# A hybrid decoder trunk on one core: the gate's product stays in PSUM, the output bias is added during the mixer, and the mixer's end is put in another order

## The chip, the core and the metric

The program runs on 1 core of one Trainium2 chip. The metric is device microseconds from the first to the last instruction and what lies around them, as the runs report it. The kernel before took 2048.25 us (median of 3 runs, 2047.78 to 2049.02).

The engines are named as the profile names them: PE is TensorE (matmuls; PEld its weight loads), DVE is VectorE, ACT is ScalarE, POOL is GpSimd, SP is SyncE. Each takes its instructions in order. DMAs are issued from SP, ACT and POOL.

## What is computed

A sequence of 256 tokens with 2048 channels, float32, goes through two layers and a final norm. The change touches only the token mixer of the first layer:

```python
def conv_module(h, w_in, b_in, dw, dw_b, ln_g, ln_b, w_out, b_out):
    u = h @ w_in + b_in
    a, gate = jnp.split(u, 2, axis=-1)
    v = a * jax.nn.sigmoid(gate)
    v = lax.conv_general_dilated(v, dw[:, None, :], ..., feature_group_count=D_MODEL) + dw_b
    v = layer_norm(v, ln_g, ln_b)
    v = jax.nn.silu(v)
    return v @ w_out + b_out
...
        if i % N_MIXERS == 0:
            x = x + conv_module(rms_norm(x, mix_norm[i]), ...)
        ...
        x = x + mlp(rms_norm(x, mlp_norm[i]), ...)
```

`w_in` is 2048 x 4096, `w_out` 2048 x 2048, and the depthwise convolution has 31 causal taps per channel. After the mixer come a dense MLP, a state-space layer with a gated output, and a second MLP.

## The kernel before

Weights are read from HBM in *steps* of 1 MB, three buffers deep (SP issues the DMAs, line 91), and a step is used in two *halves*. Each half is split into two float32r parts, `hi` on ScalarE (line 117) and `lo = raw - hi` on GpSimd or VectorE (line 119), with four buffers of each; `run_steps` writes the split of half h + 4 ahead of the products of half h. `after(n, fn)` puts work n halves later; `tick` counts.

**Input projection and gate.** `conv_in` makes 16 channel blocks c of 128 channels, four halves each. TensorE accumulates values and gate of a block, feature-major, in a PSUM tile `acc` (two of them), 24 products of 256 columns a half (`mm_g`, lines 204 to 206). From block 2 on the `lo` parts are GpSimd's. When a block is complete, `gate` (lines 419 to 431) multiplies by the token scale into an SBUF tile `ga` (VectorE, 424), takes the sigmoid in place (ScalarE, 425), and multiplies into the tile `vT` (VectorE, 426):

```python
nc.vector.tensor_tensor(out=t, in0=A, in1=self.rstdB.broadcast_to([P, 2, T]), op=ALU.mult)
nc.scalar.activation(t[:, 1, :], t[:, 1, :], AF.Sigmoid, bias=b_in[:, KB + c:KB + c + 1])
nc.vector.scalar_tensor_tensor(out=self.cblk(c), in0=t[:, 0, :], scalar=b_in[:, c:c + 1], in1=t[:, 1, :], ...)
```

**Depthwise taps.** Blocks 0 to 11 are convolved on VectorE, 30 instructions of 256 columns each (line 792 through `depthwise`, accumulator `cv` in PSUM), the first tap on ScalarE (498). Blocks 12 to 15 are *packed*: four shifted copies of the block (tile `R`, by DMA through HBM for 12 to 14, by 16 on-chip copies on lines 445 and 447 for 15) against tap matrices `wpk`, 32 small products a block on TensorE (463), result `pk`. `packed_taps` makes the tap matrices: 16 small copies into `dp` on VectorE (369), then one GpSimd product a block (376).

**Norm.** With a shift taken from blocks 0 to 3, the blocks are centred in groups of four (VectorE, 543), squared (ScalarE, 545), and summed over channels by small products into `stat` (TensorE, 510). `ln_totals` and `ln_finish` make mean and scale, hold TensorE with dummy products (`keep_warm`, line 184), and write the normalised blocks `z` and, through SiLU, the split pair `sT` (lines 604 to 610, `lo` on line 231) for the output projection.

**Output projection.** `conv_out` streams `w_out` (`mm_t`, lines 215 to 217). Ahead of its first half stands `pre`: `ln_finish`, then the bias `b_out` is loaded by one POOL DMA (624) and added to the residual x by four GpSimd instructions (627), and background work for the state-space layer is queued.

**What sets the order.** The instructions of each engine are put in order when the program is built, by a scheduler that goes by priority and its own estimates; `high_priority(URGENT)` puts one ahead, `behind(ins)` keeps one after another. On the chip every engine works that order off and waits at its head. The tags `t2` (three buffers), `ga`, `acc` and the 2 KB banks `ms` are shared by what carries them.

## Time and profile before

| | us |
|---|---|
| median of 3 runs | 2048.25 (2047.78 to 2049.02) |
| the profiled execution, its own time | 2047.59 |
| its span, first to last instruction | 2045.3 |
| TensorE busy in the span | 1991.8 (97%) |
| VectorE busy | 1426.7 (70%) |
| ScalarE busy | 943.5 (46%) |
| GpSimd busy | 325.9 (16%) |
| mean granted TensorE clock | 0.989 |

Matmuls are pipelined and their ends are modelled, so TensorE's busy share runs high: what is to be read is where it is idle, and what ended the idle time. [...] In lists of instructions the idle time of the engine just ahead of one stands in brackets, with the instruction that released it.

### The profile page before, as it was taken

To read this page: it belongs to the slowest core of one execution; us is meant where nothing else is said; L and a number is where in the kernel's file an instruction comes from. 1 tells how busy PE (TensorE), PEld (TensorE's weight loads), DVE (VectorE), ACT (ScalarE), POOL (GpSimd) and SP (SyncE) were. 2 spreads that over 40 slices of the span, in tenths; PEclk is the share of its full clock that TensorE was granted. 3 is DMA by queue.
4 is the path that set the end of the run, shared out by engine and by line. 5 is a ranking of instruction groups with operands and counts; after the bars stand their busy time and mean duration, and the time that the engine had idled before them with its cause. 6 is when DMAs were issued, how large, how long until landed. Compare 5 with 4: busy or idle time off the path is not lost.

```text
span 2045.3 us, 28886 instructions
## 1 busy us (share of the span) xinstructions
PE 1991.8 (97%) x11612; PEld 1695.5 (83%) x11612; DVE 1426.7 (70%) x1897; ACT 943.5 (46%) x1155; POOL 325.9 (16%) x266
## 2 busy tenths in 40 slices
PE   8999899999999999999998899999999999999998
PEld 8999687888888888888886688888888888888887
DVE  7999899976867777776558645566555555655555
ACT  4444455454444545454443354455444444544444
POOL 2988401100000212321013500000000000000000
PEclk9999999999999999999998899999999999999999
DMA  8667357766765778777898756665656566565653
GB/s 233 166 166 212 122 184 239 240 220 191 250 204 188 198 222 266 255 249 217 315 322 278 273 184 186 187 184 186 192 191 193 185 186 195 191 210 186 188 196 130
DMA packets 317301, 428.48 MB, mean 209 GB/s; under 512 B 10209, under 2 KB 211985, under 8 KB 313681
## 3 DMA queue, kind: packets, MB, share of 16 engines
q1 hardware_dynamic: 301120, 384.85, 60.0%
q0 software_dynamic: 12048, 37.41, 6.0%
q10 hardware_dynamic: 4000, 4.38, 0.7%
q8 instruction: 91, 1.49, 0.3%
q14 instruction: 42, 0.34, 0.0%
HBM read 400.08 MB, written 34.91 MB: 213 GB/s over the span
## 4 chain that ended last, share of the span: by engine, by line
PE 84%; DVE 12%; issue 2%; POOL 1%; DMA 1%; ACT 0%; SPq 0%; ACTq 0%; POOLq 0%; DVEq 0%
PE acc L194 23%; PE acc L215 15%; PE acc L217 14%; PE acc L216 14%; PE acc L195 11%; DVE cv L792 4%; PE acc L205 1%; PE acc L206 1%; PE acc L204 1%; DVE lo L119 1%; DVE S L783 1%; DVE vT L426 1%; DVE ws L783 1%; DMA raw<-in_conv_w_in_dram 0%; DVE wt L783 0%
## 5 line engine op out<-in xcount | busy, mean ns | idle before, releaser
L117 ACT ACTIVATE hi<-raw 128x1024 fp32r<-128x1024 f32 x672 | 711.5, 1060 | 960.0 <-PE acc L217 501.6
L119 DVE TENSOR_TENSOR lo<-raw,hi 128x1024 fp32r<-128x1024 f32 x596 | 729.1, 1224 | 520.1 <-ACT hi L117 519.3
L194 PE MATMUL acc<-hT,hi 128*128 128x512 f32 x2048 | 725.9, 399 | 3.8 <-DVE t L771 3.8
L195 PE MATMUL acc<-hT,lo 128*128 128x256 f32 x2048 | 575.5, 281 | 1.7 <-DVE lo L119 1.7
L194 PEld LDWEIGHTS acc<-hT,hi 128*128 128x128 f32 x2048 | 385.1, 188 | 99.4 <-issue 3.5
L195 PEld LDWEIGHTS acc<-hT,lo 128*128 128x128 f32 x2048 | 387.7, 189 | 3.2 <-DVE lo L119 2.3
L215 PE MATMUL acc<-hi,rT 128*128 128x512 f32 x992 | 387.5, 391 | 0.0
L216 PE MATMUL acc<-lo,rT 128*128 128x512 f32 x992 | 386.3, 389 | 0.0
L217 PE MATMUL acc<-hi,rT 128*128 128x512 f32 x992 | 386.2, 389 | 0.0
L215 PEld LDWEIGHTS acc<-hi,rT 128*128 128x128 f32 x992 | 186.2, 188 | 40.4 <-issue 1.8
L217 PEld LDWEIGHTS acc<-hi,rT 128*128 128x128 f32 x992 | 186.2, 188 | 39.1
L216 PEld LDWEIGHTS acc<-lo,rT 128*128 128x128 f32 x992 | 186.2, 188 | 38.1
L119 POOL TENSOR_TENSOR lo<-raw,hi 128x1024 fp32r<-128x1024 f32 x76 | 188.3, 2492 | 99.4 <-ACT hi L117 99.3
L204 PE MATMUL acc<-hT,hi 128*128 128x256 f32 x512 | 146.6, 287 | 1.4 <-ACT hi L117 1.4
L206 PE MATMUL acc<-hT,lo 128*128 128x256 f32 x512 | 146.0, 285 | 1.9 <-POOL lo L119 1.9
L205 PE MATMUL acc<-hT,hi 128*128 128x256 f32 x512 | 146.7, 287 | 0.0
L792 DVE SCALAR_TENSOR_TENSOR cv<-vT,dw,cv 128x256 f32<-128x256 f32 x348 | 142.1, 478 | 0.8
L783 DVE TENSOR_TENSOR x<-x,acc 128x1024 f32<-128x1024 f32 (+1 forms) x72 | 83.5, 1160 | 33.4 <-PE acc L217 23.0
L204 PEld LDWEIGHTS acc<-hT,hi 128*128 128x128 f32 x512 | 99.1, 194 | 4.2 <-issue 2.1
L206 PEld LDWEIGHTS acc<-hT,lo 128*128 128x128 f32 x512 | 99.2, 194 | 3.0 <-POOL lo L119 2.1
L215 PE MATMUL acc<-hi,yT 128*128 128x512 f32 x256 | 100.9, 394 | 0.0
L217 PE MATMUL acc<-hi,yT 128*128 128x512 f32 x256 | 100.4, 392 | 0.0
(265 smaller groups left out, 1778.2 us busy)
## 6 DMA issues: line engine op xcount, KB each, us to landing
raw<-in_mlp_w_up_dram SPq DMA_DIRECT2D x128, 1024.0 KB, 5.8
raw<-in_mlp_w_down_dram SPq DMA_DIRECT2D x128, 1024.0 KB, 5.2
raw<-in_ssm_w_glu_dram SPq DMA_DIRECT2D x32, 1024.0 KB, 5.5
raw<-in_conv_w_in_dram SPq DMA_DIRECT2D x60, 512.0 KB, 5.5
raw<-in_conv_w_out_dram SPq DMA_DIRECT2D x16, 1024.0 KB, 5.3
Vd<-bv POOLq DMA_DIRECT2D x16, 512.0 KB, 5.6
Md<-Kd POOLq DMA_DIRECT2D x32, 256.0 KB, 8.0
Wt<-Wd SPq DMA_DIRECT2D x8, 1024.0 KB, 7.8
```

What stands on the lines that cost most here:

```text
L117: self.nc.scalar.activation(hi, sl, AF.Copy)
L119: ins = eng.tensor_tensor(out=lo, in0=sl, in1=hi.bitcast(F32), op=ALU.subtract)
L194: mm(accs[m], lhsT=hi[:, kk, c], rhs=x, start=first and kk == 0, stop=False)
L195: mm(accs[m][:, 0:T], lhsT=lo[:, kk, c], rhs=x[:, 0, :], start=False, stop=last and kk == 3)
L204: mm(accs[m], lhsT=hi[:, kk, c], rhs=x[:, 0, :], start=first and kk == 0, stop=False)
L205: mm(accs[m], lhsT=hi[:, kk, c], rhs=x[:, 1, :], start=False, stop=False)
L206: mm(accs[m], lhsT=lo[:, kk, c], rhs=x[:, 0, :], start=False, stop=last and kk == 3)
L215: mm(acc[:, b, :], lhsT=ak[:, 0, t], rhs=hi[:, kk, :], start=first and kk == 0, stop=False)
L216: mm(acc[:, b, :], lhsT=ak[:, 0, t], rhs=lo[:, kk, :], start=False, stop=False)
L217: self.mm_last = mm(acc[:, b, :], lhsT=ak[:, 1, t], rhs=hi[:, kk, :], start=False, stop=last and kk == 1)
L783: self.nc.vector.tensor_tensor(out=out, in0=a, in1=b, op=op)
L792: return self.nc.vector.scalar_tensor_tensor(out=out, in0=a, scalar=s, in1=b, op0=op0, op1=op1)
```

## The change

- `gate` writes the scaled product back to its PSUM tile `acc`; the sigmoid goes from there to a tile `ga` of one block in SBUF, and the last instruction reads one operand from PSUM and one from SBUF.
- The 16 copies into `dp` go to ScalarE.
- The output bias is loaded in four pieces of 512 columns (tag `t2`) and added by GpSimd during the input projection, written at halves 20, 28, 36 and 44 (`add_b_out`), instead of ahead of the output projection.
- The 16 copies of block 15 are put in another order, six on ScalarE and ten on VectorE (before: ten and six), and go ahead of other work.
- Packed block 13 is written 8 halves after its gate, as block 12 is, instead of at the end. Block 14 and 15 stay at the end.
- Each packed block is evacuated and centred in one VectorE instruction; its square goes to ScalarE, and its two statistics products stand between the first 20 and the last 12 products of the next packed block. The centring of blocks 12 to 14 as a group goes. `ln_totals` stands within block 15's products.
- Dummy products: 3 and 9 instead of 5 and 11.

```diff
@@ packed_taps
+        self.sqs = {}
                 for g in range(4):
-                    nc.vector.tensor_copy(out=dp[32 * r:32 * r + 32, :, g, :],
-                                          in_=self.dw[32 * g:32 * g + 32, PACKED[0]:, r::4])
+                    nc.scalar.activation(dp[32 * r:32 * r + 32, :, g, :],
+                                         self.dw[32 * g:32 * g + 32, PACKED[0]:, r::4], AF.Copy)
...
+        for i in range(NS):
+            self.after(20 + 8 * i, lambda i=i: self.add_b_out(i))
+
+    def add_b_out(self, n):
+        nc = self.nc
+        s = slice(n * 512, (n + 1) * 512)
+        bo = self.t2([P, 512], name="bo")
+        nc.gpsimd.dma_start(out=bo, in_=self.a["conv_b_out"][:, s].broadcast_to([P, 512]))
+        with self.behind(self.pool_ins):
+            nc.gpsimd.tensor_tensor(out=self.x[:, :, s], in0=self.x[:, :, s],
+                                    in1=bo.unsqueeze(1).broadcast_to([P, NB, 512]), op=ALU.add)
@@ gate
-        t = self.tmp.tile([P, 2, T], F32, tag="ga", name="ga", bufs=2)
+        t = self.tmp.tile([P, T], F32, tag="ga", name="ga", bufs=2)
         with self.tc.high_priority(offset=URGENT):
-            nc.vector.tensor_tensor(out=t, in0=A, in1=self.rstdB.broadcast_to([P, 2, T]), op=ALU.mult)
-            nc.scalar.activation(t[:, 1, :], t[:, 1, :], AF.Sigmoid, bias=b_in[:, KB + c:KB + c + 1])
-            nc.vector.scalar_tensor_tensor(out=self.cblk(c), in0=t[:, 0, :], scalar=b_in[:, c:c + 1], in1=t[:, 1, :],
+            nc.vector.tensor_tensor(out=A, in0=A, in1=self.rstdB.broadcast_to([P, 2, T]), op=ALU.mult)
+            nc.scalar.activation(t, A[:, 1, :], AF.Sigmoid, bias=b_in[:, KB + c:KB + c + 1])
+            nc.vector.scalar_tensor_tensor(out=self.cblk(c), in0=A[:, 0, :], scalar=b_in[:, c:c + 1], in1=t,
                                            op0=ALU.add, op1=ALU.mult)
@@ depthwise_packed
-            for r in range(4):
-                for g in range(4):
+            for g in range(4):
+                for r in range(4):
...
-                    if (4 * r + g) % 3:
-                        nc.scalar.activation(o, v, AF.Copy)
-                    else:
-                        nc.vector.tensor_copy(out=o, in_=v)
+                    with self.tc.high_priority(offset=URGENT):
+                        if (4 * g + r) % 8 in (1, 4, 7):
+                            nc.scalar.activation(o, v, AF.Copy)
+                        else:
+                            nc.vector.tensor_copy(out=o, in_=v)
...
-            if last:
-                self.stt(self.cblk(c), ps, dwb, self.shift, ALU.add, ALU.subtract)
-            else:
-                nc.scalar.activation(self.cblk(c), ps, AF.Identity, bias=dwb)
-
-        def run(q=8):
-            ps = self.acc2(f"pk{c}")[:, 0, 0:T] if i % 2 else self.bank([P, T], name=f"pk{c}")
-            products(ps, 0, q)
-            if q < 8:
-                self.ln_feed(c - 1)
-                products(ps, q, 8)
+            self.stt(self.cblk(c), ps, dwb, self.shift, ALU.add, ALU.subtract)
+            if not last:
+                sq = self.sqs[c] = self.t2([P, T], name="sq")
+                nc.scalar.activation(sq, self.cblk(c), AF.Square)
+
+        def feed(c):
+            sq = self.sqs.pop(c)
+            for h, v in enumerate((self.cblk(c), sq)):
+                self.colsum(self.stat[:, h, :], (c,), lambda i: v, h == 0)
+
+        def run():
+            ps = self.acc2(f"pk{c}")[:, 0, 0:T] if i % 2 else self.bank([P, T], name=f"pk{c}")
+            products(ps, 0, 5)
+            if i:
+                feed(c - 1)
+            if last:
+                self.ln_totals()
+            products(ps, 5, 8)
             finish(ps)
-            if c < KB - 2:
-                self.ln_feed(c)
-        if i == 0:
+        if i < 2:
             self.after(8, run)
...
-            run(5)
+            run()
@@ ln_feed
-        g = range(c // 4 * 4, min(c // 4 * 4 + 4, KB - 1))
+        g = range(c // 4 * 4, c // 4 * 4 + 4)
...
-        elif c < PACKED[0]:
-            self.after(2, lambda: self.centre(g[0], 4))
         else:
-            self.centre(g[0], len(g))
-            self.ln_totals()
+            self.after(2, lambda: self.centre(g[0], 4))
@@ ln_finish
-        self.keep_warm(5, ins)
+        self.keep_warm(3, ins)
...
-        self.keep_warm(11, self.bc)
+        self.keep_warm(9, self.bc)
@@ conv_out, pre
-            bo = self.blk_tile([P, D], name="bo")
-            self.nc.gpsimd.dma_start(out=bo, in_=self.a["conv_b_out"].broadcast_to([P, D]))
-            for n in range(NS):
-                s = slice(n * 512, (n + 1) * 512)
-                self.nc.gpsimd.tensor_tensor(out=self.x[:, :, s], in0=self.x[:, :, s],
-                                             in1=bo[:, s].unsqueeze(1).broadcast_to([P, NB, 512]), op=ALU.add)
```

**How the order moves.** Lines behind the edits are ten to sixteen higher in the changed kernel (line 792 is 802 there, 119 stays).

ScalarE at the start of the mixer, before: from the first gate's sigmoid (425) on, with the first tap of a block (498) and the weight parts (117).

```order
L425 ACT_TABLE_LOAD
L425 ACTIVATE ga<-ga,vecs 128x256
L498 ACTIVATE cv<-vT,vecs,dw 128x256
L117 ACTIVATE hi<-raw 128x1024 x3
L425 ACTIVATE ga<-ga,vecs 128x256
```

And now, the sigmoid on line 438, the first tap on 517:

```order
L438 ACT_TABLE_LOAD
L438 ACTIVATE ga<-acc,vecs 128x256
L370 ACTIVATE dp<-dw 32x4x8 x7
L517 ACTIVATE cv<-vT,vecs,dw 128x256
L370 ACTIVATE dp<-dw 32x4x8 x9
L117 ACTIVATE hi<-raw 128x1024 x3
L438 ACTIVATE ga<-acc,vecs 128x256
```

The 16 copies now stand on ScalarE, around the first tap of block 0 and ahead of three weight parts.

GpSimd during the input projection, before: `lo` parts (119) and the tap matrices (376), then the norm's power (587), and the bias.

```order
L119 TENSOR_TENSOR lo<-raw,hi 128x1024 x8
L376 TENSOR_TENSOR wpk<-dp,m_244 128x1024
L119 TENSOR_TENSOR lo<-raw,hi 128x1024 x24
L587 TENSOR_TENSOR rstd<-lv,mhalf 128x2
L624 DMA bo<-in_conv_b_out_dram 128x2048
L840 DMA bb<-in_ssm_b_re_dram 128x1024
L841 DMA bb<-in_ssm_b_im_dram 128x1024
L627 TENSOR_TENSOR x<-x,bo 128x2x512 x4
```

And now, from the first bias piece to the third add; behind these come five `lo` parts, the last tap matrix, three more, and the fourth add:

```order
L389 DMA bo<-in_conv_b_out_dram 128x512
L119 TENSOR_TENSOR lo<-raw,hi 128x1024 x2
L389 DMA bo<-in_conv_b_out_dram 128x512
L391 TENSOR_TENSOR x<-x,bo 128x2x512
L119 TENSOR_TENSOR lo<-raw,hi 128x1024 x2
L391 TENSOR_TENSOR x<-x,bo 128x2x512
L389 DMA bo<-in_conv_b_out_dram 128x512
L119 TENSOR_TENSOR lo<-raw,hi 128x1024
L377 TENSOR_TENSOR wpk<-dp,m_244 128x1024
L119 TENSOR_TENSOR lo<-raw,hi 128x1024
L389 DMA bo<-in_conv_b_out_dram 128x512
L119 TENSOR_TENSOR lo<-raw,hi 128x1024 x2
```

Every bias piece is issued some `lo` parts ahead of its add, and the adds stand between the weight parts of blocks 7 to 11.

VectorE at the last gate, before: the gate (424, 426) of block 15 with taps (792) and centring (543) of older blocks behind it.

```order
L424 TENSOR_TENSOR ga<-acc,bcs 128x512
L792 SCALAR_TENSOR_TENSOR cv<-vT,dw,cv 128x256 x3
L426 SCALAR_TENSOR_TENSOR vT<-ga,vecs 128x256
L792 SCALAR_TENSOR_TENSOR cv<-vT,dw,cv 128x256 x2
L447 COPY R<-vT 32x284 x6
L792 SCALAR_TENSOR_TENSOR cv<-vT,dw,cv 128x256 x6
L792 SCALAR_TENSOR_TENSOR vT<-vT,dw,cv 128x256
L792 SCALAR_TENSOR_TENSOR cv<-vT,dw,cv 128x256 x3
L543 TENSOR_TENSOR vT<-vT,shift 128x3x256
L792 SCALAR_TENSOR_TENSOR vT<-vT,dw,cv 128x256
L543 TENSOR_TENSOR vT<-vT,shift 128x4x256
L792 SCALAR_TENSOR_TENSOR vT<-pk_2827,vecs,shift 128x256
```

And now, from the last taps on (gate on 437 and 439, copies on 461, centring on 559, evacuations on 802 from `pk`):

```order
L802 SCALAR_TENSOR_TENSOR vT<-vT,dw,cv 128x256
L559 TENSOR_TENSOR vT<-vT,shift 128x4x256
L802 SCALAR_TENSOR_TENSOR vT<-pk_2723,vecs,shift 128x256
L437 TENSOR_TENSOR acc<-acc,bcs 128x2x256
L439 SCALAR_TENSOR_TENSOR vT<-acc,vecs,ga 128x256
L461 COPY R<-vT 32x284 x10
L802 SCALAR_TENSOR_TENSOR vT<-pk_2811,vecs,shift 128x256
L797 TENSOR_SCALAR stat<-stat 128x256
L802 SCALAR_TENSOR_TENSOR vT<-pk_2849,vecs,shift 128x256
```

All taps, the last centring and the evacuation of block 13 (`pk_2723`) stand ahead of the last gate, and the ten copies directly behind it.

TensorE at the end of the projection, now: block 13 stands 24 products ahead of the projection's end, blocks 14 (`pk_2811`) and 15 (`pk_2849`) behind it, with the statistics (529) among them.

```order
L477 MATMUL pk_2811<-R,wpk 32x256 x2
L529 MATMUL stat<-vT,ones 32x256 x4
L477 MATMUL pk_2811<-R,wpk 32x256 x5
L529 MATMUL stat<-sq,ones 32x256 x4
L529 MATMUL stat<-vT,ones 32x256
L529 MATMUL stat<-sq,ones 32x256
L477 MATMUL pk_2811<-R,wpk 32x256 x13
L529 MATMUL stat<-vT,ones 32x256
L529 MATMUL stat<-sq,ones 32x256
L477 MATMUL pk_2811<-R,wpk 32x256 x12
L477 MATMUL pk_2849<-R,wpk 32x256 x20
L529 MATMUL stat<-vT,ones 32x256
```

Before, blocks 13, 14 and 15 stood behind the projection's end one after another, and fourteen statistics products behind all of them.

## Rows read from the trace of the kernel before

**Rows 1.** Chain that ended last, whole span: share of each engine.

```profile
PE 84%; DVE 12%; issue 2%; POOL 1%; DMA 1%; ACT 0%; SPq 0%; ACTq 0%; POOLq 0%; DVEq 0%
```

**Rows 2.** Stretches: length, busy PE, PEld, DVE, ACT, POOL (instructions), granted clock, DMA share, GB/s.

```profile
50.00:55.00 5.00, 2.91 (x23) 2.50 (x21) 4.93 (x13) 4.20 (x6) 2.12 (x1) 1.00 0.02 5
55.00:60.00 5.00, 4.70 (x26) 4.71 (x27) 5.00 (x14) 0.64 (x1) 5.00 (x4) 0.66 0.16 44
...
235.00:245.00 10.00, 9.51 (x63) 8.10 (x58) 4.88 (x11) 3.02 (x9) 2.34 (x4) 0.76 0.33 124
245.00:255.00 10.00, 5.68 (x23) 4.00 (x22) 10.00 (x9) 5.74 (x10) 9.58 (x4) 0.93 0.22 87
300.00:410.00 110.00, 104.31 (x542) 87.93 (x541) 109.33 (x155) 53.09 (x68) 14.24 (x9) 0.97 0.76 235
```

**Rows 3.** Timeline of VectorE, 28 to 62 us: start, length, instruction.

```profile
34.74 7.21 DVE L369 COPY dp<-dw 32x32 f32<-32x32 f32 x15
...
49.21 0.69 DVE L424 TENSOR_TENSOR ga<-acc,bcs 128x512 f32<-128x512 f32 x1
```

**Rows 4.** Timeline of ScalarE, 46 to 60 us, idle time ahead in brackets.

```profile
49.94 0.51 ACT L425 ACTIVATE ga<-ga,vecs 128x256 f32<-128x256 f32 x1 [8.01 <-DVE ga L424]
...
51.76 3.88 ACT L117 ACTIVATE hi<-raw 128x1024 fp32r<-128x1024 f32 x4
```

**Rows 5.** Line 426, all sixteen: shortest, median and longest in ns.

```profile
L426 DVE SCALAR_TENSOR_TENSOR vT<-ga,vecs x16: 476/1548/2503, 33.9 to 219.0; 128x256 f32<-128x256 f32 x16
```

**Rows 6.** Timeline of VectorE, 150 to 185 us: a run of taps.

```profile
157.56 7.92 DVE L792 SCALAR_TENSOR_TENSOR cv<-vT,dw,cv 128x256 f32<-128x256 f32 x20
```

**Rows 7.** Timeline of GpSimd, 144 to 164 us.

```profile
145.80 2.09 POOL L376 TENSOR_TENSOR wpk<-dp,m 128x1024 f32<-128x1024 f32 x1
...
157.81 2.41 POOL L119 TENSOR_TENSOR lo<-raw,hi 128x1024 fp32r<-128x1024 f32 x1 [0.45 <-ACT hi L117]
```

**Rows 8.** Timeline of GpSimd, 230 to 256 us: the bias DMA's issue and the adds.

```profile
240.03 0.64 POOL L624 DMA_DIRECT2D bo<-in_conv_b_out_dram  x1
...
245.42 10.12 POOL L627 TENSOR_TENSOR x<-x,bo 128x1024 f32<-128x1024 f32 x4 [3.70 <-DMA bo<-in_conv_b_out_dram]
```

**Rows 9.** DMA issues, 235 to 260 us: KB, median us to landing.

```profile
bo<-in_conv_b_out_dram POOLq DMA_DIRECT2D x1, 1024.0 KB, 5.3
```

**Rows 10.** Timeline of TensorE, 216.6 to 232 us: projection's end and packed blocks.

```profile
216.63 7.11 PE L463 MATMUL pk<-R,wpk 128*32 128x256 f32 x128
```

**Rows 11.** Timeline of ScalarE, 217 to 228 us: the last weight part.

```profile
216.68 1.06 ACT L117 ACTIVATE hi<-raw 128x1024 fp32r<-128x1024 f32 x1 [0.72 <-PE acc L205]
```

**Rows 12.** Timeline of VectorE, 216.9 to 246 us: end of the last gate.

```profile
219.03 2.50 DVE L426 SCALAR_TENSOR_TENSOR vT<-ga,vecs 128x256 f32<-128x256 f32 x1
...
245.25 2.95 DVE L231 TENSOR_TENSOR sT<-z,sT 128x256 fp32r<-128x256 f32 x2
```

**Rows 13.** Tile R, 195 to 232 us: VectorE's copies, shortest, median, longest in ns.

```profile
L447 DVE COPY R<-vT x6: 298/300/1696, 222.2 to 225.3; 32x284 f32<-32x284 f32 x6
```

**Rows 14.** Timeline of TensorE, 230 to 246 us: statistics to first output product.

```profile
233.67 1.08 PE L510 MATMUL stat<-sq,ones 128*32 128x256 f32 x8 [0.42 <-ACT sq L545]
...
236.95 1.06 PE L561 MATMUL lst<-q,stat 128*128 128x1 f32 x8 [0.49 <-ACT stat L555]
...
245.28 0.48 PE L215 MATMUL acc<-hi,sT 128*128 128x512 f32 x1
```

**Rows 15.** Timeline of TensorE, 200 to 262 us: products of the output projection.

```profile
248.25 0.51 PE L217 MATMUL acc<-hi,sT 128*128 128x512 f32 x1 [0.87 <-DVE sT L231]
...
253.36 0.67 PE L217 MATMUL acc<-hi,sT 128*128 128x512 f32 x1 [3.46 <-DVE sT L231]
...
255.53 0.63 PE L216 MATMUL acc<-lo,sT 128*128 128x512 f32 x1
...
257.34 0.39 PE L215 MATMUL acc<-hi,sT 128*128 128x512 f32 x1
```

**Rows 16.** Waits of SP's DMA queue, 0 to 260 us: total, times, longest.

```profile
SPq L91 <- POOL lo L119: 158.6, 30, 13.2
```

More of the change, by code (lines that the diff above doesn't have):

```diff
@@ L522, in ln_feed @@
             self.after(2, self.ln_shift)
-        elif c < PACKED[0]:
+        else:
             self.after(2, lambda: self.centre(g[0], 4))
-        else:
-            self.centre(g[0], len(g))
-            self.ln_totals()
     def ln_shift(self):
```

## The prediction

> **What bounds the kernel now.** I read the chain of waits first: TensorE holds 84% of it and VectorE 12% [rows 1]. Weights stream at TensorE's pace nearly everywhere, so only a TensorE wait that goes, or a new one, moves the end. Next came the busy time by stretch, for where TensorE rests [rows 2]: about 50 to 60 us, 235 to 255 us, and a little at 300 to 410 us, where VectorE is busy 109.33 of 110 us. The change touches the first two. Last I read each engine's timeline there.
>
> The first loss: VectorE copies the taps of the packed blocks, 15 of 16 in 7.21 us, and only then comes to the second gate at 49.21 [rows 3]. ScalarE stands in order behind that gate: sigmoid at 49.94, the next weight part at 51.76 [rows 4]. [...]
>
> The second loss is the end of the mixer, from the last product of the input projection (216.6) to the first of the output projection (245.28) [rows 10, 14], 28.7 us. Then the output projection waits twice more for VectorE [rows 15].
>
> **The change, part by part.** The profiled execution took 2047.59 us (span 2045.3), 0.66 under the median of 2048.25; a difference found in it is taken off the median.
>
> (a) *Tap copies to ScalarE.* Sixteen copies leave VectorE. On ScalarE I bound one between 0.2 us (an estimate, half of a one-block sigmoid's 0.51 [rows 4]) and 0.5 us, so 3 to 8 us, 4 likely. It stands idle 8.01 us before that sigmoid [rows 4], which covers them; without that cover the next weight parts would be late by what is left over. The second gate then follows its products, and the stall goes: 2.4 us idle plus (1 - 0.66) x 4.70 = 1.6 us of clock [rows 2]. Gain 4.0 us; ends 2 and 4.5.
>
> (b) *Gate product in PSUM.* The gate's last instruction takes 476 ns at best, 1548 as a median, 2503 at most [rows 5]. It reads two SBUF operands; GpSimd is working beside it. The taps, with one SBUF operand and one in PSUM, hold 7.92 us for 20, 0.39 each, through the same GpSimd work [rows 6]. So the wait is for GpSimd and goes when one operand stays in PSUM: (1.548 - 0.476) x 16 = 17 us of VectorE time. It is hidden beside TensorE until the last gate, and there it shows as the 2.50 us instruction [rows 12]; what it buys is that the tap backlog ends before that gate and not, as now, after it. [...]
>
> (c) *Output bias in the mixer.* Four adds of 10.12/4 = 2.53 us leave the output projection [rows 8]. Now GpSimd holds them from 245.42 to 255.5, and VectorE's two small subtractions take 2.95 us; TensorE waits 0.87 and 3.46 us and then runs eight products at 0.63 us instead of 0.39 [rows 8, 12, 15], 0.2 us of pitch each, 1.6 us. That is 5.9 us; I take off 0.5, since the next pair of blocks would then only just be in time: gain 5.4, ends 4 and 6.5.
>
> They go where GpSimd has 0.45 us free per 2.41 us weight part [rows 7]. The order puts 4 adds, 3 DMA issues (0.64 us [rows 8]) and 2 tap-block products (2.09 us [rows 7]) among 14 weight parts: 10.1 + 1.9 + 4.2 = 16.2 us, of which 14 x 0.45 = 6.3 is spare. Four buffers give a lead: a part's pitch is 2.86 us, it is begun three parts ahead of use and needs 1.06 us on ScalarE [rows 11] and 2.41 here, so 5.0 us. Left over: 4.9 us of TensorE wait at most, 0 at least (TensorE is itself late there by its statistics products). I take 2.5, the middle. Each DMA's landing, 5.3 us [rows 9], is covered by two weight parts ahead of its add; without that cover it is a rival below.
>
> (d) *Packed block 13 ahead of the projection's last half.* Two blocks are 128 records (two a product) in 7.11 us, 3.6 us a block [rows 10]: the projection ends 3.6 us later and the tail has one block less. By itself 0.
>
> (e) *The tail, from the projection's end E.* Last weight part on ScalarE 1.06 [rows 11], sigmoid 0.51, gate end 0.48, handovers 0.15: 2.2 us. VectorE's ten copies find GpSimd in its last weight part (to 1.06 + 0.1 + 2.41 = 3.5) and wait for it, as the longest now does (1696 ns), then 0.33 each [rows 13]: E + 6.8. Block 14 and twelve statistics products (eight records, four products, took 1.08 us, 0.27 each [rows 14]: 3.2 us) fill TensorE to about the same point. Block 15 with two more statistics: 3.6 + 0.5, E + 10.9. From there to the first output product the steps are those of now, 236.95 to 245.28, 8.3 us [rows 14]; centring and statistics of blocks 12 to 14 no longer stand ahead of it. E + 19.2 against 28.7: 9.5 us less, of which (d) takes 3.6: gain 5.9. Ends: VectorE 3 us late at the last gate, or the copies unhindered: 3 and 8.
>
> (f) ScalarE loses three evacuations and gains squares; VectorE gains three evacuations of 0.5 us: hidden in its 17 us. [...] SP's order is unchanged. Later orders differ only in how VectorE's background work is interleaved up to about 410 us: 0, ends -2 and +2.
>
> Sum: 4.0 + 5.4 - 2.5 + 5.9 = 12.8 us. 2048.25 - 12.8 = 2035.4, about **2035**. Ends of the terms, not all at once, give 5 to 18 us.
>
> **The rivals.**
> *GpSimd behind.* The weight parts are late by all that is uncovered, twice over if VectorE's centring passes hold GpSimd as well: some 9 us instead of 2.5, 2042. For it: the 0.45 us margin; against: single tap-block products are absorbed today.
> [...]
> *Absorbed.* The stretch at 300 to 410 us is VectorE's (109.33 of 110 us [rows 2]), and if its work there kept its place in time, TensorE would only wait longer: 2047.5. Against: that work is queued behind the mixer's end and starts with it.
> *Slower.* Place: the GpSimd queue in the mixer. If each bias DMA is waited for in full (its buffer, one of three shared, freed late, so the issue slips next to its add), 4 x 5.3 = 21 us [rows 9] join a queue that is already full. TensorE waits them out, and SP's loads, which wait for these same parts (158.6 us in 30 waits [rows 16]), leave no way to catch up: 2035 + 21 = 2056. It decides against the change once over 15 us stay uncovered (12.8 and the 2.5 already counted). Against: the order keeps two parts between issue and add for the first two bias pieces, and more for the others.
> That the gate's wait stays in spite of PSUM I count with GpSimd behind: the backlog would then end after the last gate again.
>
> **How the numbers follow.** About 0.2%, 4.1 us, is what a measurement here tells from no change. Forecast 0.61 (2030 to 2040), GpSimd behind 0.13, cold start 0.10: faster 0.84. Absorbed 0.09: same. Slower 0.07. The range 2029 to 2043 holds the first three with their bounds and leaves out the other two, 0.16, and a little on the far side.
>
> **What would show it.** Right: no TensorE rest at 50 to 60 us and a granted clock near 1 there; the gate's end near 0.48 us every time; TensorE waits on GpSimd parts of 0 to 5 us between 100 and 180 us; last tap ahead of the last gate; 18 to 21 us from the projection's last product to the first output product, and that product near 238; no wait over 1 us in the first output slice. Wrong: weight-part waits over 10 us in the mixer, VectorE reaching the last gate over 3 us after its products, or a TensorE rest at 300 to 410 us well over today's 5.7 us.

## The result, and the profile of the changed kernel

The changed kernel took 2030.26 us (median of 4 runs, 2028.35 to 2030.84) against 2048.64 us (4 runs, 2047.78 to 2049.33): ratio 0.9904, 95% interval 0.9889 to 0.9919. Faster, as forecast, but by 18 to 20 us where 13 were forecast. The ratio times the 2048.25 us of the forecast gives 2028.6, 0.4 us under the low end of the range. The profiled execution of the changed kernel took 2028.35 us, span 2026.1.

The chain that ended last, whole span, after [rows 1]: VectorE's share fell from 12% to 4%.

```profile
PE 92%; DVE 4%; DMA 1%; issue 1%; SPq 0%; POOL 0%; ACT 0%; ACTq 0%; POOLq 0%; DVEq 0%
```

Busy time by stretch, after, with the columns of [rows 2]:

```profile
50.00:55.00 5.00, 5.00 (x44) 5.00 (x43) 4.73 (x13) 1.98 (x3) 5.00 (x3) 1.00 0.87 228
55.00:60.00 5.00, 5.00 (x44) 5.00 (x43) 4.47 (x13) 2.03 (x3) 4.56 (x3) 1.00 0.83 226
...
235.00:245.00 10.00, 9.46 (x40) 7.52 (x41) 9.97 (x16) 9.94 (x19) 0.00 (x0) 1.00 0.01 2
245.00:255.00 10.00, 10.00 (x45) 8.28 (x45) 9.91 (x15) 6.38 (x9) 3.03 (x4) 1.00 0.81 242
...
300.00:410.00 110.00, 103.80 (x563) 88.49 (x562) 108.68 (x148) 52.59 (x69) 10.21 (x10) 0.97 0.81 254
```

TensorE no longer rests at 50 to 60 us, the granted clock at 55 to 60 us is 1.00 instead of 0.66 (before, it was 0.50 from 56.0 to 58.5 us and 1.00 from 59.0 us on), and at 235 to 255 us TensorE is busy 19.5 of 20 us instead of 15.2. The stretch at 300 to 410 us has kept its character. TensorE's timeline, after, 222 to 240 us, with the idle time ahead in brackets; [rows 14, 15] are its counterpart:

```profile
222.58 2.86 PE L477 MATMUL pk<-R,wpk 128*32 128x256 f32 x43 [0.54 <-DVE R L461]
...
234.26 0.50 PE L215 MATMUL acc<-hi,sT 128*128 128x512 f32 x1 [0.25 <-ACT sT L230]
235.23 0.50 PE L217 MATMUL acc<-hi,sT 128*128 128x512 f32 x1 [0.23 <-DVE sT L231]
...
238.56 0.50 PE L217 MATMUL acc<-hi,sT 128*128 128x512 f32 x1 [0.31 <-DVE sT L231]
```

TensorE starts the first output product at 234.26 instead of 245.28, and the waits of 0.87 and 3.46 us behind it are 0.23 and 0.31. Line 439, the gate's last instruction, after [rows 5], as shortest, median and longest of the sixteen:

```profile
L439 DVE SCALAR_TENSOR_TENSOR vT<-acc,vecs,ga x16: 477/482/494, 33.1 to 217.7; 128x256 f32<-128x256 f32 x16
```

Where TensorE is at the same point of the program in the two profiled executions tells where the 19.2 us came from:

| point of the program | before | after | lead | forecast of the step |
|---|---|---|---|---|
| 8th half of the projection | 37.85 | 37.04 | 0.8 | 0 |
| 14th half, behind the second gate | 59.53 | 54.32 | 5.2 | (a) +4.0, found +4.4 |
| 63rd half | 210.78 | 206.58 | 4.2 | (c) -2.5, found -1.0 |
| projection's end | 216.70 | 216.28 | 0.4 | (d) -3.6, found -3.8 |
| first output product | 245.28 | 234.26 | 11.0 | (d, e) +9.5, found +10.6 |
| end of the output projection | 346.43 | 330.24 | 16.2 | (c) +5.4, found +5.2 |
| end of the first MLP's first slice | 445.90 | 427.14 | 18.8 | (f) 0, found +2.6 |
| last instruction | 2045.3 | 2026.1 | 19.2 | 0, found +0.4 |

### The profile page after: what moved, and what is told of

It reads as the page before. It is cut to its first block, busy times and chain, and to the rows that moved or that the text cites. A ratio compares the mean times of both kernels' runs of the same rounds, so it can differ in the third digit from the quotient of the medians.

```text
span 2026.1 us, 28879 instructions
## 1 busy us (share of the span) xinstructions
PE 1985.1 (98%) x11604; PEld 1691.6 (83%) x11604; DVE 1399.7 (69%) x1887; ACT 946.0 (47%) x1166; POOL 320.2 (16%) x269
## 4 chain that ended last, share of the span: by engine, by line
PE 92%; DVE 4%; DMA 1%; issue 1%; SPq 0%; POOL 0%; ACT 0%; ACTq 0%; POOLq 0%; DVEq 0%
PE acc L194 24%; PE acc L215 15%; PE acc L217 15%; PE acc L216 15%; PE acc L195 12%; PE acc L204 3%; PE acc L206 3%; PE acc L205 3%; DMA raw<-in_conv_w_in_dram 1%; DVE lo L119 1%; PE pk L477 1%; DMA R<-Rd 1%; DVE S L793 1%; SPq L91 0%; PE kp L1086 0%
## 5 line engine op out<-in xcount | busy, mean ns | idle before, releaser
L195 PEld LDWEIGHTS acc<-hT,lo 128*128 128x128 f32 x2048 | 387.4, 189 | 1.5 <-DVE lo L119 0.7
L793 DVE TENSOR_TENSOR x<-x,acc 128x1024 f32<-128x1024 f32 (+1 forms) x72 | 83.7, 1163 | 33.3 <-PE acc L217 22.9
L216 PE MATMUL acc<-lo,yT 128*128 128x512 f32 x256 | 99.9, 390 | 0.0
```

What stands on the lines that cost most here:

```text
L195: mm(accs[m][:, 0:T], lhsT=lo[:, kk, c], rhs=x[:, 0, :], start=False, stop=last and kk == 3)
L216: mm(acc[:, b, :], lhsT=ak[:, 0, t], rhs=lo[:, kk, :], start=False, stop=False)
L793: self.nc.vector.tensor_tensor(out=out, in0=a, in1=b, op=op)
```

## The experiments

The kernel before ranged from 2044 to 2056 us in these jobs, so each ratio is to its runs in the same job; 0.001 of ratio is 2.05 us.

### One edit at a time

The kernel before with one edit of the change each: copies into `dp` on ScalarE (A), gate product in PSUM (B), output bias in the mixer (C), and the mixer's end with its fewer dummy products (D).

```diff
# A_only
-                    nc.vector.tensor_copy(out=dp[...], in_=self.dw[...])
+                    nc.scalar.activation(dp[...], self.dw[...], AF.Copy)
# B_only
-            nc.vector.tensor_tensor(out=t, in0=A, ...)
+            nc.vector.tensor_tensor(out=A, in0=A, ...)
...
# C_only
+            self.after(20 + 8 * i, lambda i=i: self.add_b_out(i))
...
# D_only
-        if i == 0:
+        if i < 2:
...
```

A:

> The kernel before with one edit: the 16 copies into dp on ScalarE. Theory (the second gate comes late behind the copies): the rest and the half-speed stretch at 50 to 60 us go, 4.4 us as read between the two traces, and nothing else changes: about 2044.2 against 2048.6, the second gate near 40 us instead of 49. Rival (the copies delay ScalarE's weight parts instead): TensorE rests elsewhere before 60 us, 2047 to 2049.

B:

> The kernel before with one edit: the gate's product in PSUM. Theory (VectorE's time in the mixer is hidden beside TensorE up to the last gate): the gate's last instruction takes 0.48 us every time, and only the last one's 2.0 us are on the path, with up to 1 us more from a shorter tap backlog: 2045 to 2047. Rival (VectorE's 17 us come out later, where VectorE is busy all the time at 300 to 410 us): 2040 to 2044, with TensorE's 11.8 us of idle time between 245 and 446 us falling by 4 us or more.

C:

> The kernel before with one edit: the output bias loaded in four pieces and added during the mixer. Theory: 5.2 us come out of the first output slice (16.2 us lead gained between the first output product and the next stage, less the 11.0 at its start, as read between the two traces), about 1 us goes back in the mixer where weight parts are late: 2044 to 2045. If the lead of the first MLP slice (2.6 us) belongs to this edit too: 2041 to 2042. Rival (the added GpSimd work holds VectorE's two-operand gates up, which here still read SBUF twice): the last gate is later by 1 to 3 us, 2045.5 to 2048.

D:

> The kernel before with the end of the mixer alone in the new order: copies, block 13, centring and statistics per block, fewer dummy products. Theory (the order needs VectorE to have its taps done before the last gate, which the other edits buy): the tail shrinks by less than 6.9 us, 3 to 5: 2043.5 to 2045.5, with the last taps still behind the last gate. Rival (the order alone is enough): 6.5 us or more, below 2042.

### Three edits without the fourth

The changed kernel with one of the four undone.

```diff
# no_act_taps: A undone; no_gate_psum: B undone; no_bias_move: C undone; no_new_end: D undone
-            nc.vector.tensor_tensor(out=A, in0=A, ...)
+            nc.vector.tensor_tensor(out=t, in0=A, ...)
...
```

A undone:

> The changed kernel with the 16 copies into dp back on VectorE. Theory: TensorE rests at 50 to 60 us again, 4.4 us: 2034 to 2035.5. Rival (with the gate in PSUM VectorE catches up and the second gate is in time): 2029.5 to 2031.5.

B undone:

> The changed kernel with the gate's product back in SBUF, all else kept. Theory (the gate's last instruction, with two SBUF operands, starts only in a gap of GpSimd's work, and the bias adds and tap matrices close those gaps between about 123 and 165 us): one gate near 130 us takes 15 to 20 us as in the run of the bias edit alone (17.4 us), TensorE runs out of weights, and the time is 2046 to 2054, no better than the kernel before. Rival (that stall came from something else in the bias edit, such as its loads, and the gate's place is worth what its own run gave, about 2 to 5 us): 2032 to 2036.

C undone:

> The changed kernel with the output bias back ahead of the output projection. Theory (5.2 us of the first output slice less 1.0 us in the mixer): 2034 to 2036, with TensorE idle 3 us or more in the first output slice, where GpSimd's adds stand beside VectorE's subtractions. Rival (GpSimd's adds were hidden there once the tail is short): 2029 to 2031.5.

D undone:

> The kernel before with the three other edits: copies into dp on ScalarE, gate product in PSUM, bias in the mixer. Theory (the new end is worth 6.9 us up to the first output product and 2.5 us in the first MLP slice, as the run of the end alone showed there): 2038 to 2041. Rival (the other edits shorten the tail already, since taps are done ahead of the last gate): 2032 to 2036.

Measured, all eight; the changes in us are the ratio's distance from 1 times 2048.6:

| edit | alone: median, ratio (95%) | us | undone: median, ratio (95%) | the edit's worth among the others |
|---|---|---|---|---|
| A | 2043.65, 0.9972 (0.9960 to 0.9983) | -5.7 | 2034.09, 0.9926 (0.9901 to 0.9950) | -4.5 |
| B | 2041.38, 0.9975 (0.9958 to 0.9991) | -5.1 | 2050.58, 1.0007 (0.9998 to 1.0017) | -21.1 |
| C | 2056.00, 1.0030 (1.0017 to 1.0044) | +6.1 | 2037.12, 0.9941 (0.9919 to 0.9963) | -7.6 |
| D | 2041.55, 0.9961 (0.9950 to 0.9972) | -8.0 | 2033.23, 0.9925 (0.9905 to 0.9945) | -4.3 |

The four alone add up to -12.7 us, all together give -19.7. The intervals are wide: in the last column only B's worth is well clear of them, and C's just touches. A and D may be worth the same either way, within their intervals. B and C are not: C alone makes the kernel slower, and without B the other three give nothing.

A, A undone and B undone came out as the theory had it. B, D and D undone fell into the range of the rival. C alone lies beyond both of its ranges, and C undone 1.1 us beyond that of its theory. B alone is not understood: its ten runs lie between 2037.94 and 2051.92 us, its profiled execution took 2048.80, and in it TensorE is idle for 15.8 us from the first output product to the end of the first MLP slice, where the rival asked for 4 us less than the 11.8 of before.

C alone and B undone have one and the same event. VectorE, GpSimd and TensorE in the run of C alone, 130 to 166 us (the gate's lines are 436 and 438 there):

```profile
132.12 1.64 DVE L798 SCALAR_TENSOR_TENSOR cv<-vT,dw,cv 128x256 f32<-128x256 f32 x4
133.68 17.40 DVE L438 SCALAR_TENSOR_TENSOR vT<-ga,vecs 128x256 f32<-128x256 f32 x1
...
134.76 2.39 POOL L390 TENSOR_TENSOR x<-x,bo 128x1024 f32<-128x1024 f32 x1
137.12 11.81 POOL L119 TENSOR_TENSOR lo<-raw,hi 128x1024 fp32r<-128x1024 f32 x5
148.90 1.90 POOL L376 TENSOR_TENSOR wpk<-dp,m 128x1024 f32<-128x1024 f32 x1
165.48 4.72 POOL L119 TENSOR_TENSOR lo<-raw,hi 128x1024 fp32r<-128x1024 f32 x2 [14.68 <-ACT hi L117]
...
165.46 0.58 PE L204 MATMUL acc<-hT,hi 128*128 128x256 f32 x1 [17.24 <-DVE cv L798]
```

GpSimd works from 130.01 to 150.80 without a gap (two weight parts stand ahead of the add), and the gate's last instruction, begun at 133.68, ends at 151.08, 0.28 us after GpSimd ran dry. It ran dry because the gate stood still: 29 taps follow on VectorE, the next gate only at 162.37, ScalarE waits for it with the next weight parts behind it, and TensorE rests 17.24 us. With B undone, first the gate's row, and behind it TensorE's at the end of the same stall:

```profile
L439 DVE SCALAR_TENSOR_TENSOR vT<-ga,vecs x16: 474/1558/17435, 35.2 to 239.1; 128x256 f32<-128x256 f32 x16
```

```profile
162.72 0.58 PE L204 MATMUL acc<-hT,hi 128*128 128x256 f32 x1 [17.25 <-ACT hi L117]
```

In the changed kernel GpSimd is as full, and the gates do not wait for it: each takes 0.48 or 0.49 us there. TensorE waits for a weight part by some tenths at most. GpSimd, after, 118 to 172 us:

```profile
125.14 4.78 POOL L119 TENSOR_TENSOR lo<-raw,hi 128x1024 fp32r<-128x1024 f32 x2
129.86 2.42 POOL L391 TENSOR_TENSOR x<-x,bo 128x1024 f32<-128x1024 f32 x1
132.22 11.87 POOL L119 TENSOR_TENSOR lo<-raw,hi 128x1024 fp32r<-128x1024 f32 x5
144.06 1.91 POOL L377 TENSOR_TENSOR wpk<-dp,m 128x1024 f32<-128x1024 f32 x1
145.93 7.13 POOL L119 TENSOR_TENSOR lo<-raw,hi 128x1024 fp32r<-128x1024 f32 x3
153.03 2.39 POOL L391 TENSOR_TENSOR x<-x,bo 128x1024 f32<-128x1024 f32 x1
155.39 18.94 POOL L119 TENSOR_TENSOR lo<-raw,hi 128x1024 fp32r<-128x1024 f32 x8
```

### Is it the full queue, or the bias edit as such?

The changed kernel with B undone, and the bias left out; and the changed kernel with the bias left out.

```diff
# sbuf_no_adds and no_adds
-            self.after(20 + 8 * i, lambda i=i: self.add_b_out(i))
# sbuf_no_adds also
-            nc.vector.tensor_tensor(out=A, in0=A, ...)
+            nc.vector.tensor_tensor(out=t, in0=A, ...)
...
```

Gate in SBUF, no adds:

> The changed kernel with the gate's product in SBUF and without the output bias (its loads and adds are left out, so the output lacks the bias). Theory (the stall of 17 us needs both: a gate with two SBUF operands, and a GpSimd queue without gaps): no gate instruction over 3 us, no stall near 145 to 163 us, 2030 to 2034. Rival (the gate in SBUF stalls with the new order of the mixer in any case): a gate instruction over 10 us, 2044 or more.

No adds:

> The changed kernel without the output bias (its loads and adds are left out, so the output lacks the bias). Theory (the adds cost what TensorE's lead lost between the 38th and 55th half, 1.0 us): 2027 to 2029.5, and 0.5 us or more between the weight parts' end and their use all through the mixer. Rival (the adds delay the gates and taps and through them the tail): 2025 to 2026.5.

Measured: 2032.42 us, ratio 0.9916 (0.9900 to 0.9932), and 2032.15 us, 0.9914 (0.9898 to 0.9929). The first one's gate, and behind it two of GpSimd's rows at the place where the stall was:

```profile
L427 DVE SCALAR_TENSOR_TENSOR vT<-ga,vecs x16: 897/1583/2245, 33.5 to 218.5; 128x256 f32<-128x256 f32 x16
```

```profile
129.97 2.42 POOL L119 TENSOR_TENSOR lo<-raw,hi 128x1024 fp32r<-128x1024 f32 x1 [0.45 <-ACT hi L117]
132.86 2.42 POOL L119 TENSOR_TENSOR lo<-raw,hi 128x1024 fp32r<-128x1024 f32 x1 [0.48 <-ACT hi L117]
```

Without the loads and adds GpSimd has its gaps of 0.45 us back, and a gate with two SBUF operands takes 2.2 us at most. So in these runs the stall came only with both: the two SBUF operands, and the bias in the mixer (17.40 and 17.43 us, against 2.25 at most without the bias and 0.49 with an operand in PSUM). That it is the closed gaps which keep the gate out is not shown, and they are not enough by themselves. In the kernel before, five parts of GpSimd stand without a gap from 188.19 on, and a gate begins in the second of them:

```profile
188.19 13.04 POOL L119 TENSOR_TENSOR lo<-raw,hi 128x1024 fp32r<-128x1024 f32 x5 [2.05 <-ACT hi L117]
190.86 2.39 DVE L426 SCALAR_TENSOR_TENSOR vT<-ga,vecs 128x256 f32<-128x256 f32 x1
```

It ends at 193.25, 0.28 us after that second part (190.56 to 192.97), though the third begins at once. The four adds of [rows 8] stand back to back too, and the second subtraction of [rows 12] ends 0.28 us after the first add. In the two stalls the gate does not get in at the end of the instruction that it began in, nor at the next ones. Both times it began in the weight part directly ahead of a bias add, which no other gate with two SBUF operands does in these runs; whether that decides it stays open.

The second run lies above both of its ranges: leaving the adds out gains nothing measurable. TensorE loses 1.0 us less between the 39th and the 63rd half, as the theory had it, but that lead is lost again at the mixer's end, where TensorE rests 2.79 us ahead of block 15 instead of 0.54, in another order of the same work.

### The end of the mixer

The changed kernel with block 15's copies as before; with block 13 behind the projection; without the dummy products.

```diff
# old_copies
-            for g in range(4):
-                for r in range(4):
+            for r in range(4):
+                for g in range(4):
...
-                        if (4 * g + r) % 8 in (1, 4, 7):
+                    if (4 * r + g) % 3:
# block13_end
-        if i < 2:
+        if i < 1:
# no_dummies
-        self.keep_warm(3, ins)
-        self.keep_warm(9, self.bc)
```

Old copies:

> The changed kernel with block 15's copies as before: ten on ScalarE, six on VectorE, without the high priority. Theory (TensorE rests 2.5 us or more ahead of block 15, and the clock falls after that rest): the stretch from the totals to the first output product takes 7.5 to 8.4 us instead of 6.9, and the first output product is 3 to 4.5 us later: 2032 to 2034. Rival (the copies are hidden beside blocks 14 and 15): 2029 to 2031.

Block 13 at the end:

> The changed kernel with packed block 13 behind the projection, as before. Theory (it only moves 3.6 us of TensorE work): projection's end 3.6 us earlier, first output product where it was within 1 us, 2028 to 2031. Rival (its evacuation, square and statistics join the tail): 1.5 to 3 us more, 2030.5 to 2033.

No dummies:

> The changed kernel without the 12 dummy products. Theory A (they keep the clock up while VectorE makes the first normalised blocks): the granted clock falls in the first output products, which take 0.2 us more each for 8 to 16 of them, 2030.5 to 2033. Theory B (what keeps it up is that TensorE did not rest ahead of the totals): same time as the changed kernel, 2028 to 2030.5, clock 1.00 up to the first output product.

Measured: 2029.26 us, 0.9904 (0.9884 to 0.9924); 2031.37 us, 0.9916 (0.9894 to 0.9939); 2036.60 us, 0.9941 (0.9924 to 0.9957). The new order of the copies is worth nothing measurable (the rest ahead of block 15 was 0.29 us with the old, so the theory's rest of 2.5 us did not come). Moving block 13 may be worth a microsecond: with it at the end, the first output product came 22.9 us behind the projection's end, where 18.0 and the block's 3.66 make 21.6; the intervals overlap. The dummy products carry weight: the intervals with and without them lie apart. Without them, TensorE's rows, and the stretches from the totals to the first output product and 12 us on:

```profile
235.59 0.80 PE L215 MATMUL acc<-hi,sT 128*128 128x512 f32 x1 [2.25 <-ACT sT L230]
...
240.57 0.63 PE L217 MATMUL acc<-hi,sT 128*128 128x512 f32 x1
...
242.14 0.39 PE L216 MATMUL acc<-lo,sT 128*128 128x512 f32 x1
```

```profile
228.68:235.59 6.91, 3.59 (x23) 2.76 (x22) 4.60 (x11) 2.44 (x7) 1.82 (x3) 0.93 0.35 122
235.59:247.59 12.00, 12.00 (x41) 9.45 (x42) 11.71 (x19) 11.55 (x21) 0.00 (x0) 0.76 0.04 17
```

The first output product comes no later behind the totals (6.91 us in both), but it comes after a rest of 2.25 us, and twelve or so products run at 0.63 us instead of 0.39, with a granted clock of 0.76 over the 12 us. The output projection is 2.6 us longer for it (98.57 against 95.98). With the 12 dummy products the same 12 us have 1.00: theory A, in its cause. To a slow start of this kind, a "cold start", the prediction gives a chance of 0.10. The time is 3.6 us above its range, because the next slice is 4.3 us longer too (101.20 against 96.90); that this hangs on the clock is not shown, since the slice takes 96.9 to 101.4 us in these kernels.

What goes with the clock in the stretch from the totals (line 577, 561 before) to the first output product is to be seen by setting kernels side by side, one row each: before, after, the run without D, B alone, A alone, and C undone.

```profile
236.95:245.28 8.33, 8.33 (x55) 8.04 (x55) 5.13 (x12) 2.86 (x8) 2.34 (x4) 0.80 0.44 165
```

```profile
227.35:234.26 6.91, 6.26 (x47) 5.75 (x46) 4.60 (x11) 2.44 (x7) 1.82 (x3) 1.00 0.35 123
```

```profile
227.75:236.14 8.39, 8.39 (x54) 8.03 (x55) 4.90 (x11) 2.60 (x8) 1.82 (x3) 0.80 0.33 125
```

```profile
232.36:242.71 10.35, 10.35 (x54) 9.94 (x55) 4.81 (x11) 2.54 (x8) 3.01 (x5) 0.63 0.42 154
```

```profile
231.50:238.38 6.88, 6.88 (x54) 6.60 (x55) 4.47 (x11) 2.29 (x7) 2.34 (x4) 1.00 0.37 127
```

```profile
228.27:235.78 7.51, 7.51 (x46) 7.11 (x47) 4.73 (x11) 2.39 (x7) 2.35 (x4) 0.77 0.35 145
```

At a granted clock of 1.00 the stretch takes 6.9 us, in every kernel that had it, with 12 dummy products or with all 16 (A alone). With 16 it takes 8.3 to 8.4 us at 0.80 and 10.4 at 0.63; with 12 it takes 7.5 at 0.77. What lowers the clock here is not shown. It is not TensorE's rests ahead of the totals by themselves: A alone rests 2.81, 0.45 and 0.49 us there, as the kernel before does (2.81, 0.42, 0.49), and has 1.00; the run without D rests 0.62, 0.41 and 0.49 us and has 0.80.

### What the bias costs ahead of the output projection

The kernel before without the bias.

```diff
-            self.nc.gpsimd.dma_start(out=bo, in_=self.a["conv_b_out"].broadcast_to([P, D]))
-                self.nc.gpsimd.tensor_tensor(out=self.x[:, :, s], in0=self.x[:, :, s], ...)
```

> The kernel before without the output bias (load and adds are left out, so the output lacks the bias). Theory (all VectorE time that the adds cost beside them comes out of the end, since VectorE is busy all the time up to 420 us): first output product up to the end of the first MLP slice 194 to 195.5 us instead of 200.6, 2041.5 to 2044. Rival (only the waits and slow products in the first output slice go, and the waits behind 300 us take them back): 197 us or more, 2045 to 2048.

Measured: 2038.17 us, 0.9950 (0.9932 to 0.9968), 10.2 us less (6.6 to 13.9), more than the theory had. The output projection and the first MLP slice, first before, then without the bias:

```profile
245.28:346.43 101.15, 94.83 (x422) 77.07 (x421) 98.31 (x186) 55.97 (x80) 17.18 (x12) 0.97 0.61 195
346.43:445.90 99.47, 94.00 (x543) 81.30 (x542) 90.95 (x123) 48.01 (x62) 11.37 (x6) 0.98 0.76 237
```

```profile
245.75:339.94 94.19, 91.64 (x422) 74.89 (x421) 90.78 (x182) 55.91 (x80) 7.04 (x8) 1.00 0.62 199
339.94:438.50 98.56, 94.62 (x542) 81.31 (x542) 91.84 (x127) 48.36 (x62) 7.42 (x6) 0.98 0.80 242
```

The two stretches together fall from 200.6 to 192.8 us, and VectorE's busy time in the first by 7.5 us: the nine subtractions of line 231 no longer stand beside GpSimd's adds, and take 5.6 us together instead of 12.1. With the bias edit alone they take 195.2 us, with the whole change 192.9; with C undone 198.7, and TensorE waits there as before:

```profile
239.18 0.50 PE L217 MATMUL acc<-hi,sT 128*128 128x512 f32 x1 [0.90 <-DVE sT L231]
...
244.28 0.61 PE L217 MATMUL acc<-hi,sT 128*128 128x512 f32 x1 [3.44 <-DVE sT L231]
```

### An attempt to go further

TensorE still rests 2.2 and 3.6 us at 311 and 359 us, for VectorE. The changed kernel with VectorE's background work spread thinner:

```diff
-            self.rate = 2.75
+            self.rate = 2.4
...
-                                self.rate = 2.75
+                                self.rate = 2.4
```

2.4:

> The changed kernel with the background work for the state-space layer spread thinner (rate 2.4 for 2.75 a half, in the output projection and in the first MLP). Theory (at 250 to 410 us VectorE is busy all the time, and TensorE's 6.2 us of idle time there and the clock after it hang on that): 2 to 5 us less than the changed kernel, 2024 to 2027. Rival (those waits come at fixed places of the program, whatever VectorE's load): 2029 to 2031.

2.0:

> As before with rate 2.0. Theory: the waits at 300 to 410 us are gone, 5 to 8 us less than the changed kernel, 2021 to 2025. Rival (the work moved out of that stretch is then late for the state-space layer behind 1000 us): 2030 or more, with TensorE idle there longer than now.

Measured: 2044.09 us, 0.9968 (0.9958 to 0.9977), and 2088.76 us, 1.0191 (1.0175 to 1.0207), both slower than the changed kernel, by 13 and 59 us. My theory fell: at 2.4 the waits at 311 and 359 us stayed (2.23 and 3.44 us). At 2.0 these two are gone, but one of 5.96 us at 391 us stands in their place, so they do not come at fixed places of the program either. The work that was pushed back is missing behind 1000 us, the rival of the second run: between 1000 and 1100 us TensorE is busy 91.4 us in the changed kernel, 84.9 at 2.4 and 60.0 at 2.0. TensorE, rate 2.4, 1025 to 1035 us, as the first of several:

```profile
1030.34 0.80 PE L215 MATMUL acc<-hi,rT 128*128 128x512 f32 x1 [4.45 <-ACT hi L117]
```

None of the kernels tried is clear of the changed one on the fast side.

## Why the prediction was right in sign and short in size

Faster was right, and so were the places. Between the two profiled executions lie 19.2 us where the sum had 12.8, so 6.4 us more. The steps that failed are terms of the sum: (f), put at 0 and found at 2.6 us; the cost of (c) in the mixer, put at 2.5 us and found at 1.0; and in (e) the steps from the totals on, carried over as 8.3 us and found at 6.9, by which the tail gave 0.9 us more in all. (a) gave 0.4 more, the gain of (c) 0.2 less, and 1.2 us lie in what no edit touches.

**(a) Taps to ScalarE: right.** 4.0 us forecast, 4.4 found, 4.5 when undone, 5.7 alone (3.5 to 8.2).

**(b) The gate's product in PSUM: the size in the sum was right, and what it is for was missed.** The wait is for GpSimd, as read from [rows 5, 6]: one operand in PSUM brings 476 to 2503 ns down to 477 to 494, and the PSUM source added nothing that the row shows. The step of it that failed is "It is hidden beside TensorE until the last gate". That does not hold together with (c). [Rows 7] show GpSimd's gaps, 0.45 us per weight part, and (c) spends exactly these, with 10.1 + 1.9 + 4.2 us of work against 6.3 spare. I had both numbers and put them into separate terms. With the bias in the mixer and two SBUF operands, one gate waits 17.4 us, until GpSimd has run dry, and everything stands behind it. This did not move the forecast of the whole change, which has both edits; it would have mispriced C alone. So (b) is worth 21 us among the others, all of the change and a little more, though it takes only some 17 us of VectorE's time, most of that hidden. The gate at 190.86 in the kernel before ended 0.28 us after the GpSimd part it began in, and took 2.39 us. In the two stalls VectorE did not get in at the end of one instruction, but after eight. Why is open.

**(c) The bias: the cost was too high, the gain about right.** 2.5 us in the mixer were forecast, 1.0 found between the 39th and the 63rd half (lead 5.2 to 4.2), and leaving the adds out gained nothing measurable. The lead that the queue starts with was larger than the 5.0 us of the sum: the weight part of the 33rd half was ready 7.1 us ahead of its use, TensorE being late by its statistics products. The gain was 5.2 us up to the end of the output projection, against 5.4.

**(d, e) The tail: the first part right, the second too long.** From the projection's end to the totals 10.9 us were forecast and 11.1 found (216.28 to 227.35). The failing term is "the steps are those of now, 236.95 to 245.28, 8.3 us": it took 6.9. Those 8.3 us were measured at a granted clock of 0.80, and the new tail had 1.00. I had counted this clock only as a chance to cost (cold start, 0.10). It gave 1.4 us, without which the tail would have been 0.5 us less than forecast. That the clock would be up there was not foreseen, and what put it up is open: the new tail has one rest of 0.54 us ahead of the totals, but a tail with the old rests had 1.00 as well (A alone). Whose gain the tail is came out otherwise too: without D the tail from the projection's end to the first output product had already shrunk from 28.6 to 24.0 us, by A, B and C together; D added 2.4 (24.0 less block 13's 3.66, against 18.0), of which 1.5 is again the stretch at the lower clock (8.39 against 6.91).

**(f) "Later orders ... 0, ends -2 and +2": too small.** The first MLP slice gave 2.6 us. It isn't tied to one edit: across the kernels that slice took 96.9 to 101.4 us, 97.0 with D alone and 101.4 with B alone, by rests of 0.3 to 5.4 us that VectorE ends and a clock of 0.97 to 1.00. What sets these is open. The remaining 1.2 us (0.8 at the start, 0.4 at the end) lie in what no edit touches; seven of the eight kernels with one or three of the edits had a lead of about 0.6 us or more at the first gate, and the eighth, B undone, was 0.8 us behind, so the 0.8 seems to belong to the single executions and not to the change.

**The rivals.** GpSimd behind: no weight part was late by more than some tenths. Absorbed: no, the two stretches behind the mixer shrank by 7.7 us with VectorE still busy 108.7 of 110. Slower: it named the right place, the GpSimd queue in the mixer, and the wrong victim. It saw weight parts late for TensorE; the runs without B show the gate late for VectorE. In the change as made, (b) keeps that away. The forecast of 2035 with 0.61 was too high by four terms that all came out on the same side, by 0.4 to 2.6 us; the range took their ends one or two at a time.

## What to carry to other kernels

Before filling the gaps of an engine, ask who lives in them. Here a VectorE instruction with two SBUF operands took 0.5 to 2.5 us beside GpSimd's weight parts, and 17.4 us once in each of two kernels with bias adds among them; with one operand in PSUM it took 0.5 us beside the same work. Terms that use the same slack aren't independent: undo each edit from the whole, and do not only try each alone. A duration taken from a stretch with a reduced clock is not the duration of that step: look at the granted clock of the row before carrying it over (here 8.3 us at 0.80 became 6.9 at 1.00). Where TensorE must rest just ahead of a long run of products, try work that is not needed: here the first 12 us of the run had a granted clock of 1.00 with 12 dummy products ahead of it, and 0.76 without.

## What was not expected of the hardware

- One VectorE instruction, 0.48 us by itself, took 17.40 and 17.43 us in two kernels, through a run of eight GpSimd instructions, and ended within 0.3 us of the last one's end. In the kernel before the same instruction took 2.50 us at most, and at 190.86 (2.39 us) it got in behind the first GpSimd instruction that it met, though the next followed at once.
- The same rests of TensorE went with different clocks: behind rests of 2.81, some 0.4 and 0.49 us the stretch from the totals on had a granted clock of 0.80 in the kernel before and 1.00 with A alone.
- A rest of 2.25 us of TensorE, without dummy products ahead of it, was followed by some 12 products at 0.63 instead of 0.39 us. With dummy products, rests of 0.23 to 0.31 us in the same place were followed by none.
